# One masked product instead of two: sliding-window attention with unsplit weights, a difference of values, and squares in halves

## The chip, the core and the metric

The kernel runs on one core of a Trainium2 chip. A core has five engines with an instruction queue each, which run side by side and wait for one another through semaphores: TensorE (matrix products; PE in the profile, and PEld for its loading of weights), VectorE (DVE), ScalarE (ACT), GpSimd (POOL) and SyncE (SP), which issues most of the DMA transfers. The metric is the device time of one execution in microseconds, the median of several runs.

## The reference

One decoder layer on 2048 tokens of width 1024, in float32. A projection of the normed input gives queries (8 heads of 64), keys and values (2 shared heads of 64) and the input of a convolution group. Attention and convolution are put side by side, projected, normed and added to the input; a SwiGLU feed-forward with its own norms follows. The part that matters here is the attention, over a window of 128 with 128-token blocks:

```python
s = jnp.einsum("bnqhgd,bnkhd->bnhgqk", qb, kb) * scale      # 128 queries x 256 keys of a block
dist = qi + BLOCK - kj
in_band = (dist >= 0) & (dist < WINDOW)
s = jnp.where(valid, s + bias, -jnp.inf)
m = jnp.maximum(jnp.max(s, axis=-1, keepdims=True), sink)
p = jnp.exp(s - m)
denom = jnp.sum(p, axis=-1, keepdims=True) + jnp.exp(sink - m)
o = jnp.einsum("bnhgqk,bnkhd->bnqhgd", p / denom, vb)
```

For query q of a block, the keys in the band are those of the same block up to q and those of the block before it after q: exactly 128 keys, one for each key position 0 to 127. So a 128 x 128 matrix of weights per head holds all of them, with a key position k that belongs to the own block where k <= q and to the previous block where k > q. The norms are x times the reciprocal root of the mean of its squares over 1024 columns.

## The kernel before

The sequence is worked through in four tiles of 512 tokens (T = 512), each of four blocks of 128 (P = 128). Generators emit the work; a run loop advances a main generator and, with each step, pumps side lanes by a credit in estimated microseconds (`Lane`, from L1260 on). The final order on each engine is then made by the tile framework's scheduler, which works with its own timeline and with priorities, so an edit in one place may move instructions in others. Within an engine, instructions run in the order in which they stand.

The stages, with the letter that marks their tiles in the profile:
- `stage_a` (A): the projections, 14 units of 128 columns for each sequence tile. Products with float32 operands are made of three matmuls on a high and a low part, so each operand is split: ScalarE copies the high part (L133, L782), GpSimd or VectorE subtracts to get the low part (L135, L85). Weights of a unit arrive in a tile `raw` of two buffers. In the first sequence tile, a sum of squares (ScalarE L282 into `wx`, one buffer; VectorE adds; a product with `ones`) gives the norm, and row norms of later tiles are summed by ScalarE at L272. At the first of the four query units, the 512 values just projected are transposed on TensorE into a PSUM bank and copied to `vtok` (L415), which has five blocks: the last block of the previous sequence tile (L414) and the four of this one.
- `stage_b` (B): attention of a sequence tile, block by block. `front(b)` makes the scores of the 256 keys, folds the two key blocks into one 128 x 128 matrix per head with a predicated copy, adds the bias, takes the maximum, and ScalarE takes the exponentials (L478). `back(b)` multiplies by the reciprocal of the sum (VectorE), transposes the weights of four heads at a time (group g; TensorE L496), ScalarE copies them to `pg[:, 1]` (L497), and GpSimd selects twice (L499): keys after the query go to `pg[:, 0]`, and the others stay in `pg[:, 1]`, in place. Four products (the `mat` of L517) then add, in one PSUM bank, `pg[:, 1]` with the block's own values for both groups and `pg[:, 0]` with those of the previous block. The first block of the sequence has no previous one.
- taps and tail of the convolution (C): 480 scalar-tensor-tensor instructions on VectorE, in a lane of low priority, and transposes, norm and a small product.
- `stage_w` and `norm_w` (W): output projection and the two norms behind it. Each norm sums squares of four rows of 1024 with ScalarE (L738, L760), which writes the squares to a tile `junk` that nobody reads and the sum to a small tile; `rsqrt` follows on VectorE and, for three of the four, on GpSimd.
- H, F and G: the feed-forward with one level of a seven-product scheme. `stage_p2` (G) reads out PSUM on VectorE between its products; `finish` sums squares in halves of 512 (L1087).

Small vectors come from pools of 16 buffers that are named by the stage's letter (`sm`, L67).

Of the kernel before, what the change touches and what calls it, by code (L numbers as in the profile page):

```python
# [37 lines left out]
def layer_kernel(ctx, tc, x, xT, cols, rows, sinks, relb, onehot, w_in, w_pw, w_out, w_gate, w_up, w_down, out):  # L38
# [28 lines left out]
    def sm(n, dt=F32):  # L67
        kind = "A" if lab[0][0] == "G" else lab[0][0]
        return sb.tile([P, 8], dt, tag="sm" + kind, name=nm("sm"), bufs=16)[:, 0:n]
# [80 lines left out]
    def rsqrt(ssq, n, mean_over, beside_taps=True):  # L150
# [16 lines left out]
        return y  # L167

    def rsqrt_one(a, b):
        v, y, w, vs = (sm(1) for _ in range(4))  # L170
        stt(v, a, EPS, b, ALU.add, ALU.add)
        vts(y.bitcast(I32), v.bitcast(I32), 1, None, ALU.logical_shift_right)
        vts(y.bitcast(I32), y.bitcast(I32), -1, 0x5F3759DF, ALU.mult, ALU.add)
        vts(vs, v, -(2.0**-13), None, ALU.mult)
        for f, d in ((v, -3.0), (v, -12.0), (vs, 3 * 2.0**-5)):
            stt(w, y, f, y, ALU.mult, ALU.mult)
            stt(y, w, d, y, ALU.add, ALU.mult)
        return y
# [27 lines left out]
    for i in range(4):  # L206
# [5 lines left out]
        x0.append(xt)  # L212
    ones = cst.tile([P, 1], F32, name="ones")
    nc.vector.memset(ones, 1.0)
# [17 lines left out]

    neg = cst.tile([P, 1], F32, name="neg")
    nc.vector.memset(neg, NEG)
# [6 lines left out]
    nc.gpsimd.memset(kz[:, :, 0:P].bitcast(F32), 0.0)  # L241
    junk = cst.tile([P, D], BF16, name="junk")
    vtok = cst.tile([P, 5, P], F32, name="vtok")

# [19 lines left out]
    def row_norms(ts, tag):  # L264
        lab[0] = f"A{ts[0]}"
        n = 4 * len(ts)
        ssq = sm(n)
        for i in range(n):
            xt = f4(tag)
            r0 = ts[0] * T + i * P  # L270
            nc.sync.dma_start(xt, x[r0 : r0 + P])
            act(junk, xt, AF.Square, accum_out=ssq[:, i : i + 1])  # L272
        r = rsqrt(ssq, n, D)
        for j, t in enumerate(ts):
            rn[t] = r[:, 4 * j : 4 * j + 4]
# [51 lines left out]
    def stage_a(t, hn, before_kv, hooks, post=None):  # L327
# [79 lines left out]
        for i in range(4):  # L407
            oq = proj(10 + i)
            if i == 0:
                pv = mm()  # L410
                for s in range(4):
                    nc.tensor.transpose(pv[:, s * P : (s + 1) * P], vt[:, s * P : (s + 1) * P], ident)
                if t:
                    nc.vector.tensor_copy(vtok[:, 0], vtok[:, 4])  # L414
                nc.vector.tensor_copy(vtok[:, 1:5].rearrange("p a b -> p (a b)"), pv)  # L415
            qi = hl("ql")
# [13 lines left out]
    def stage_b(t):  # L430
# [54 lines left out]
        def back(b):  # L485
# [3 lines left out]
            for g in range(2):  # L489
# [7 lines left out]
                act(pg[:, 1], o, AF.Copy)  # L497
                for kb in range(1 if first else 0, 2):
                    nc.gpsimd.affine_select(  # L499
                        out=pg[:, kb].rearrange("p (i q) -> p i q", q=P),  # L500
                        in_=pg[:, 1].rearrange("p (i q) -> p i q", q=P),
                        compare_op=ALU.is_ge if kb else ALU.is_gt,
                        fill=0.0,
                        base=0,
                        pattern=[[0, 4], [1 if kb else -1, P]],
                        channel_multiplier=-1 if kb else 1,
                    )
# [6 lines left out]
            for kb in (1,) if first else (1, 0):  # L514
                for g in (1, 0):
                    sl = slice(64 * g, 64 * g + 64)
                    r = mat(o[sl], vtok[:, b + kb, sl], pt[g][:, kb], start=kb == 1, stop=first or kb == 0)  # L517
                    if lead is None:
                        lead = r
                    else:  # L520
                        after_first(lead, r)
# [111 lines left out]
    def stage_x():  # L633
        lab[0] = "X0"
        rel = cst.tile([32, 8], F32, name="rel")
        nc.sync.dma_start(rel, relb)
# [95 lines left out]
    def norm_w(w, spill, acc, mtag):  # L732
        L = f"W{w}"
        lab[0] = L
        gb = load_gb(0)
        ssq = sm(4)
        for s in range(4):
            act(junk, acc[s], AF.Square, accum_out=ssq[:, s : s + 1])  # L738
            yield 0.5
            lab[0] = L  # L740
        r = rsqrt(ssq, 4, D, w < 3)
        yield 3
        lab[0] = L
        ssq2 = sm(4)
        for s in range(4):
# [13 lines left out]
            nc.sync.dma_start(h_scr[r0 : r0 + P], acc[s])  # L759
            act(junk, acc[s], AF.Square, accum_out=ssq2[:, s : s + 1])  # L760
            yield 1.5
        lab[0] = L
        r2 = rsqrt(ssq2, 4, D, w < 3)
        yield 3
# [316 lines left out]
    def finish(L, gb, jobs, pool=True):  # L1081
# [3 lines left out]
        for j, (rows_, halves) in enumerate(jobs):  # L1085
            for n in range(2):
                act(junk[:, 0:T], halves[n], AF.Square, scale=D**-0.5, accum_out=ssq[:, 2 * n + j : 2 * n + j + 1])  # L1087
                vtt(halves[n], halves[n], gb[n], ALU.mult)
            yield 2.0
            lab[0] = L  # L1090
# [12 lines left out]
    def stage_p2(ws, am, td, last=False):  # L1103
# [60 lines left out]
        def scale_even(h):  # L1164
            for b in (2 * h, 2 * h + 1):
                lab[0] = L
                c = home("c11", "x", b)
                act(junk[:, 0:T], c, AF.Square, scale=D**-0.5, accum_out=sse[:, b : b + 1])
                ptt(c, c, gbs[0], ALU.mult)
# [68 lines left out]
        for b in range(4):  # L1238
# [3 lines left out]
            ssq = sm(1)  # L1242
            act(junk[:, 0:T], banks[b], AF.Square, scale=D**-0.5, accum_out=ssq)
            g = f2("fa")
# [245 lines left out]
```

## Time and profile before

| what | value |
|---|---|
| median of 3 runs | 2036.23 us (2028.73 to 2038.02) |
| profiled execution, its own time | 2033.91 us |
| its span, first to last instruction | 2032.2 us |
| mean granted TensorE clock | 0.987 |
| busy: TensorE, VectorE, ScalarE, GpSimd | 1959.0, 1504.8, 988.8, 382.4 us |

The attention lies between about 95 and 600 us of the span. A busy time is the sum of the engine's instructions and not yet a place on the path: since TensorE is busy for nearly all of the span, what the time depends on is where TensorE waits and for whom, and at what clock it runs. The rows that show it stand in the prediction. In a row of the timeline, the first numbers are start and duration in microseconds, and the brackets say how long the engine was idle before and what ended it.

### The profile page before, as it was taken

To read this page: it belongs to the slowest core of one execution; us is meant where nothing else is said; L and a number is where in the kernel's file an instruction comes from. 1 tells how busy PE (TensorE), PEld (TensorE's weight loads), DVE (VectorE), ACT (ScalarE), POOL (GpSimd) and SP (SyncE) were. 2 spreads that over 40 slices of the span, in tenths; PEclk is the share of its full clock that TensorE was granted. 3 is DMA by queue.
4 is the path that set the end of the run, shared out by engine and by line. 5 is a ranking of instruction groups with operands and counts; after the bars stand their busy time and mean duration, and the time that the engine had idled before them with its cause. 6 is when DMAs were issued, how large, how long until landed. Compare 5 with 4: busy or idle time off the path is not lost. (4 is left out here: it accounts for less than half of the span.)

```text
span 2032.2 us, 27181 instructions
## 1 busy us (share of the span) xinstructions
PE 1959.0 (96%) x8826; PEld 1566.8 (77%) x8826; DVE 1504.8 (74%) x2664; ACT 988.8 (49%) x1938; POOL 382.4 (19%) x447
## 2 busy tenths in 40 slices
PE   8999999998889989999989999989999999999998
PEld 7877767776667778788878878878788888888886
DVE  5999887993895889888649985576756665545557
ACT  5455445456546633333346457556643433345443
POOL 6011224423111300000001012102523233221000
PEclk9999999999999999999999999999999999999999
DMA  8786645568558876777376778589944443266554
GB/s 310 268 290 234 207 129 187 189 221 276 184 174 305 291 236 235 271 248 255 133 265 208 231 251 297 188 285 335 335 154 161 150 171 115 98 228 230 193 187 165
DMA packets 234110, 451.44 MB, mean 222 GB/s; under 512 B 23496, under 2 KB 49264, under 8 KB 233968
## 3 DMA queue, kind: packets, MB, share of 16 engines
q1 hardware_dynamic: 211184, 411.96, 60.7%
q10 hardware_dynamic: 20544, 30.42, 4.1%
q0 software_dynamic: 2240, 7.34, 0.9%
q8 instruction: 69, 1.13, 0.2%
q14 instruction: 73, 0.60, 0.1%
HBM read 330.60 MB, written 119.02 MB: 221 GB/s over the span
## 5 line engine op out<-in xcount | busy, mean ns | idle before, releaser
L85 DVE SCALAR_TENSOR_TENSOR fc@C<-glu@C,colt,fc@C 128x512 f32<-128x512 f32 x480 | 371.7, 788 | 3.0
L108 PE MATMUL mm@F<-hl@H,w@F 128*128 128x512 f32 x1056 | 254.3, 392 | 3.1 <-ACT mm@F L909 3.1
L108 PE MATMUL mm@G<-hl@G,hl@G 128*128 128x512 f32 x924 | 229.1, 398 | 6.0 <-DVE x@G L85 5.3
L108 PEld LDWEIGHTS mm@F<-hl@H,w@F 128*128 128x128 f32 x1056 | 198.8, 189 | 45.6 <-ACT mm@F L909 4.0
L108 PEld LDWEIGHTS mm@G<-hl@G,hl@G 128*128 128x128 f32 x924 | 174.9, 192 | 43.9 <-ACT hl@G L782 5.9
L108 PE MATMUL mm@A<-hl@A,w@A 128*128 128x512 f32 x840 | 205.8, 396 | 2.3 <-DVE hl@A L85 1.2
L782 ACT ACTIVATE w@F<-chl@F 128x512 fp32r<-128x512 f32 x220 | 135.5, 625 | 145.3 <-PE mm@F L108 139.7
L108 PE MATMUL mm@G<-w@G,hl@G 128*128 128x512 f32 x876 | 199.5, 389 | 0.0
L108 PEld LDWEIGHTS mm@G<-w@G,hl@G 128*128 128x128 f32 x876 | 164.4, 188 | 34.1
L108 PEld LDWEIGHTS mm@A<-hl@A,w@A 128*128 128x128 f32 x840 | 154.9, 188 | 37.4 <-DVE hl@A L85 3.1
L85 DVE TENSOR_TENSOR w@F<-chl@F,w@F 128x512 fp32r<-128x512 f32 x198 | 146.6, 742 | 38.8 <-ACT w@F L782 38.2
L108 PE MATMUL mm@F<-mid@H,w@F 128*128 128x512 f32 x528 | 133.7, 398 | 4.7 <-ACT mm@F L909 3.4
L108 PE MATMUL mm@F<-p@H,w@F 128*128 128x512 f32 x528 | 130.8, 393 | 0.3 <-ACT at@F L1031 0.3
L108 PE MATMUL mm@F<-ql@H,w@F 128*128 128x512 f32 x528 | 127.4, 390 | 2.5 <-ACT w@F L782 2.2
L108 PE MATMUL mm@F<-x@H,w@F 128*128 128x512 f32 x528 | 125.8, 391 | 1.5 <-ACT fa@F L931 1.5
L108 PEld LDWEIGHTS mm@F<-mid@H,w@F 128*128 128x128 f32 x528 | 100.1, 191 | 27.6 <-ACT mm@F L909 4.0
L108 PEld LDWEIGHTS mm@F<-ql@H,w@F 128*128 128x128 f32 x528 | 98.9, 188 | 23.9 <-ACT w@F L782 2.8
L108 PEld LDWEIGHTS mm@F<-p@H,w@F 128*128 128x128 f32 x528 | 100.0, 190 | 22.0 <-ACT at@F L1031 1.1
L108 PEld LDWEIGHTS mm@F<-x@H,w@F 128*128 128x128 f32 x528 | 98.7, 188 | 22.7 <-ACT fa@F L931 1.9
L133 ACT ACTIVATE w@A<-raw@A 128x512 fp32r<-128x512 f32 x110 | 67.3, 626 | 88.4 <-PE mm@A L108 46.5
L108 PE MATMUL mm@W<-w@W,hl@W 128*128 128x512 f32 x384 | 100.4, 405 | 8.3 <-ACT hl@W L704 6.3
L108 PE MATMUL tr@W<-w@W,ql@W 128*128 128x512 f32 x384 | 98.8, 396 | 6.0 <-ACT mid@W L675 4.8
(299 smaller groups left out, 3368.3 us busy)
## 6 DMA issues: line engine op xcount, KB each, us to landing
mids<-fa@F SPq DMA_DIRECT2D x154, 256.0 KB, 2.6
raw@A<-w_in SPq DMA_DIRECT2D x55, 512.0 KB, 4.5
w@A<-lo_in SPq DMA_DIRECT2D x84, 256.0 KB, 3.5
fc@G<-mids SPq DMA_DIRECT2D x77, 256.0 KB, 3.4
fa@G<-mids SPq DMA_DIRECT2D x75, 256.0 KB, 4.4
gb@F<-keeps SPq DMA_DIRECT2D x72, 256.0 KB, 4.3
raw@W<-w_out SPq DMA_DIRECT2D x32, 512.0 KB, 5.4
w@W<-lo_out SPq DMA_DIRECT2D x48, 256.0 KB, 3.8
```

The lines of the kernel that those rows point to most:

```text
L85: r = op(*args, **kw)
L108: r = nc.tensor.matmul(*args, **kw)
L133: act(w[:, 0], raw, AF.Copy)
L782: act(w[:, 0], x, AF.Copy)
```

## The change

- Attention: the transposed weights stay whole in `pg[:, 1]`, and only one select is left, of the keys after the query into `pg[:, 0]`. The products are: all weights with the block's own values, plus the selected weights with the difference of the previous block's values and the own ones. `vtok` shrinks to the four blocks of the tile, and `vdif` holds the four differences; the first of them is made from the last block of the previous tile.
- `norm_w`: each sum of squares is made in two halves of 512 columns, and a VectorE add joins the two sets of four sums. `junk` shrinks to 512 columns. The row norms write their squares over their own input, which nobody reads afterwards.
- Smaller moves: `ones` and `neg` share a tile, `rel` becomes one of the small vectors, and these of stage X come from the pool of A.

```diff
     def sm(n, dt=F32):
-        kind = "A" if lab[0][0] == "G" else lab[0][0]
+        kind = "A" if lab[0][0] in "GX" else lab[0][0]
...
+    def squares(row, to, s):
+        for n in range(2):
+            act(junk, row[:, n * T : (n + 1) * T], AF.Square, accum_out=to[:, 4 * n + s : 4 * n + s + 1])
+
+    def joined(s):
+        o = sm(4)
+        vtt(o, s[:, 0:4], s[:, 4:8], ALU.add)
+        return o
...
-    ones = cst.tile([P, 1], F32, name="ones")
+    ones_neg = cst.tile([P, 2], F32, name="ones_neg")
+    ones, neg = ones_neg[:, 0:1], ones_neg[:, 1:2]
...
-    junk = cst.tile([P, D], BF16, name="junk")
-    vtok = cst.tile([P, 5, P], F32, name="vtok")
+    junk = cst.tile([P, T], BF16, name="junk")
+    vtok = cst.tile([P, 4, P], F32, name="vtok")
+    vdif = cst.tile([P, 4, P], F32, name="vdif")
...
             nc.sync.dma_start(xt, x[r0 : r0 + P])
-            act(junk, xt, AF.Square, accum_out=ssq[:, i : i + 1])
+            act(xt, xt, AF.Square, accum_out=ssq[:, i : i + 1])
...
                 if t:
-                    nc.vector.tensor_copy(vtok[:, 0], vtok[:, 4])
-                nc.vector.tensor_copy(vtok[:, 1:5].rearrange("p a b -> p (a b)"), pv)
+                    nc.vector.tensor_copy(vdif[:, 0], vtok[:, 3])
+                nc.vector.tensor_copy(vtok.rearrange("p a b -> p (a b)"), pv)
+                if t:
+                    vtt(vdif[:, 0], vdif[:, 0], vtok[:, 0], ALU.subtract)
+                vtt(vdif[:, 1:], vtok[:, 0:3], vtok[:, 1:], ALU.subtract)
...
                 act(pg[:, 1], o, AF.Copy)
-                for kb in range(1 if first else 0, 2):
+                if not first:
                     nc.gpsimd.affine_select(
-                        out=pg[:, kb].rearrange("p (i q) -> p i q", q=P),
+                        out=pg[:, 0].rearrange("p (i q) -> p i q", q=P),
                         in_=pg[:, 1].rearrange("p (i q) -> p i q", q=P),
-                        compare_op=ALU.is_ge if kb else ALU.is_gt,
+                        compare_op=ALU.is_gt,
                         fill=0.0,
                         base=0,
-                        pattern=[[0, 4], [1 if kb else -1, P]],
-                        channel_multiplier=-1 if kb else 1,
+                        pattern=[[0, 4], [-1, P]],
+                        channel_multiplier=1,
                     )
...
-                    r = mat(o[sl], vtok[:, b + kb, sl], pt[g][:, kb], start=kb == 1, stop=first or kb == 0)
+                    r = mat(o[sl], vtok[:, b, sl] if kb else vdif[:, b, sl], pt[g][:, kb], start=kb == 1, stop=first or kb == 0)
...
-        rel = cst.tile([32, 8], F32, name="rel")
+        rel = sm(8)[0:32]
...
-        ssq = sm(4)
+        ssq = sm(8)
         for s in range(4):
-            act(junk, acc[s], AF.Square, accum_out=ssq[:, s : s + 1])
+            squares(acc[s], ssq, s)
             yield 0.5
             lab[0] = L
-        r = rsqrt(ssq, 4, D, w < 3)
+        r = rsqrt(joined(ssq), 4, D, w < 3)
...
-            act(junk, acc[s], AF.Square, accum_out=ssq2[:, s : s + 1])
+            squares(acc[s], ssq2, s)
             yield 1.5
         lab[0] = L
-        r2 = rsqrt(ssq2, 4, D, w < 3)
+        r2 = rsqrt(joined(ssq2), 4, D, w < 3)
```

More of the change, by code (lines that the diff above doesn't have):

```diff
@@ L231, in layer_kernel @@
     h_scr = dr.tile([S, D], F32, name="h_scr")
-    neg = cst.tile([P, 1], F32, name="neg")
     nc.vector.memset(neg, NEG)
@@ L735, in norm_w @@
         gb = load_gb(0)
-        ssq = sm(4)
+        ssq = sm(8)
         for s in range(4):
-            act(junk, acc[s], AF.Square, accum_out=ssq[:, s : s + 1])
+            squares(acc[s], ssq, s)
             yield 0.5
             lab[0] = L
-        r = rsqrt(ssq, 4, D, w < 3)
+        r = rsqrt(joined(ssq), 4, D, w < 3)
         yield 3
         lab[0] = L
-        ssq2 = sm(4)
+        ssq2 = sm(8)
         for s in range(4):
@@ L1086, in finish @@
             for n in range(2):
-                act(junk[:, 0:T], halves[n], AF.Square, scale=D**-0.5, accum_out=ssq[:, 2 * n + j : 2 * n + j + 1])
+                act(junk, halves[n], AF.Square, scale=D**-0.5, accum_out=ssq[:, 2 * n + j : 2 * n + j + 1])
                 vtt(halves[n], halves[n], gb[n], ALU.mult)
@@ L1167, in scale_even @@
                 c = home("c11", "x", b)
-                act(junk[:, 0:T], c, AF.Square, scale=D**-0.5, accum_out=sse[:, b : b + 1])
+                act(junk, c, AF.Square, scale=D**-0.5, accum_out=sse[:, b : b + 1])
                 ptt(c, c, gbs[0], ALU.mult)
@@ L1242, in stage_p2 @@
             ssq = sm(1)
-            act(junk[:, 0:T], banks[b], AF.Square, scale=D**-0.5, accum_out=ssq)
+            act(junk, banks[b], AF.Square, scale=D**-0.5, accum_out=ssq)
             g = f2("fa")
```

## The prediction

> **What bounds the kernel now.** I read the page's shares of busy time first, then the waits of TensorE, then the windows and the timeline around the largest of them.
>
> ```profile
> span 2032.2 us, 27181 instructions
> PE 1959.0 (96%) x8826; PEld 1566.8 (77%) x8826; DVE 1504.8 (74%) x2664; ACT 988.8 (49%) x1938; POOL 382.4 (19%) x447
> ```
> TensorE is busy for 1959.0 of 2032.2 us. Its instructions stay the same in number and shape here, so only two things can move the time: the 73 us in which it idles, and stretches in which its granted clock is low. The waits of TensorE (us in total, times, longest) say who holds it:
>
> ```profile
> PE tr@B L108 <- POOL p@B L499: 10.4, 4, 6.8
> PE mm@F L108 <- ACT mm@F L909: 6.5, 4, 2.5
> PE mm@W L108 <- ACT hl@W L704: 6.3, 5, 3.0
> PE mm@G L108 <- DVE x@G L85: 5.3, 1, 5.3
> ```
> The largest is the one that the change touches: the product of weights and values waits for GpSimd's selects. Two of its four waits hold nearly all of it (instructions in order of time; start, duration, engine):
>
> ```profile
> 277.80 0.60 PE L496 MATMUL tr@B<-ident,p@B 128*128 128x128 f32 x4
> 283.43 0.57 ACT L497 ACTIVATE p@B<-tr@B 128x512 f32<-128x512 f32 x1
> 284.08 1.71 POOL L499 TENSOR_SCALAR_AFFINE_SELECT p@B<-p@B 128x512 f32<-128x512 f32 x2 [5.84 <-ACT p@B L497]
> 285.83 2.81 PE L108 MATMUL tr@B<-p@B,vtok 128*64 128x512 f32 x8 [3.08 <-POOL p@B L499]
> ```
> ```profile
> 453.96 0.49 PE L496 MATMUL tr@B<-ident,p@B 128*128 128x128 f32 x3
> 455.52 1.08 ACT L497 ACTIVATE p@B<-tr@B 128x512 f32<-128x512 f32 x2
> 456.19 7.50 POOL L499 TENSOR_SCALAR_AFFINE_SELECT p@B<-p@B 128x512 f32<-128x512 f32 x4 [5.45 <-ACT p@B L497]
> 456.75 1.29 DVE L85 TENSOR_TENSOR x@W<-fa@W,x@W 128x512 f32<-128x512 f32 x2
> 457.95 1.22 DVE L85 TENSOR_TENSOR x@W<-wx@W,x@W 128x1024 f32<-128x1024 f32 x1
> 463.74 3.68 PE L108 MATMUL tr@B<-p@B,vtok 128*64 128x512 f32 x8 [6.77 <-POOL p@B L499]
> ```
> Transposes, ScalarE's copy, the selects, then the product: in the first case the copy comes late, in the second four selects take 7.50 us. A long wait costs a second time, through the clock (window, TensorE busy, ..., granted clock in the third column from the end):
>
> ```profile
> 1750.00:1800.00 50.00, 50.00 (x223) 41.39 (x222) 22.12 (x30) 19.59 (x36) 12.97 (x10) 1.00 0.35 121
> 286.00:292.00 6.00, 6.00 (x27) 2.95 (x26) 5.89 (x7) 2.42 (x4) 2.91 (x2) 0.72 0.57 181
> 464.00:468.00 4.00, 4.00 (x13) 1.02 (x12) 0.92 (x2) 3.04 (x8) 1.27 (x1) 0.54 1.02 406
> ```
> An undisturbed matmul takes 50/223 = 0.224 us. Behind the two waits the clock is 0.72 for 6 us and 0.54 for 4 us: 1.7 + 1.8 = 3.5 us lost.
>
> **The change, part by part.**
>
> *Selects and the wait.*
> ```profile
> L499 POOL TENSOR_SCALAR_AFFINE_SELECT p@B<-p@B 128x512 f32<-128x512 f32 x62 | 59.5, 968 | 214.0 <-ACT p@B L497 212.7
> L499 POOL TENSOR_SCALAR_AFFINE_SELECT p@B<-p@B x62: 632/868/5287, 129.4 to 592.2; 128x512 f32<-128x512 f32 x62
> ```
> 32 of 62 selects go (31 us of GpSimd, off the path). What counts: the first two of the four products now need ScalarE's copy alone, the last two one select per group instead of two. The order of the built programs also moves: counting the instructions between a block's last transpose and its product at 0.224 us, most blocks had 7 to 10 us of other TensorE work there and now have 5 to 7; the two bad ones go from 4.3 to 6.7 us (286) and from 2.5 to 5.9 us (464), up to the masked pair. So, by the rows above: at 286 the copy ends at 284.0 and one select of 0.86 at 284.9; the masked pair stands at 278.4 + 6.7 = 285.1: no wait. At 464 the four selects took 7.50; three at the median 0.74 leave 5.3 for the first (the group's maximum), so the second group's one select ends at about 456.2 + 5.3 + 0.7 = 462.2, and the pair stands at 454.45 + 5.9 = 460.4: 1.8 us of wait stay. A block that had cover enough before loses some:
>
> ```profile
> 368.74 0.60 PE L496 MATMUL tr@B<-ident,p@B 128*128 128x128 f32 x4
> 375.38 0.58 ACT L497 ACTIVATE p@B<-tr@B 128x512 f32<-128x512 f32 x1
> 376.04 1.67 POOL L499 TENSOR_SCALAR_AFFINE_SELECT p@B<-p@B 128x512 f32<-128x512 f32 x2 [1.78 <-ACT p@B L497]
> ```
> Its unsplit pair stands 6.1 us behind 369.3, at 375.4, and the copy ends at 376.0: 0.6 us. The other blocks give about 1.0 us together. Taken: -10.4 + (1.8 + 0.6 + 1.0) = -7.0, and since no wait over 3 us is left, -3.5 of clock. Bounds: 0 (all waits come back) and -13.9.
>
> The Trainium skill (TensorE: Matmul & The Clock Gate, "What's actually happening") says that the array falls to half clock after an idle window of about 3.4 us and returns after as long a busy one. The trace agrees at 464 (0.54), but shows a drop at 286 already behind 3.08 us. By the rule that second drop was chance and the clock term would be 1.8 instead of 3.5.
>
> *The difference of values.*
> ```profile
> L415 DVE COPY vtok<-mm@A x4: 680/688/692, 82.5 to 468.6; 128x512 f32<-128x512 f32 x4
> L414 DVE COPY vtok<-vtok x3: 212/220/220, 90.9 to 386.4; 128x128 f32<-128x128 f32 x3
> ```
> Per sequence tile one subtract of 384 columns (between 0.22 and 0.69; 0.55) and one of 128 (0.22) from the second tile on: 2.9 us of VectorE. The copy keeps its place, and so does its wait for the previous tile's last product, in front of the taps in VectorE's queue. The first product comes 60 us behind the first copy, so nothing reaches TensorE: 0 (at most +2.9).
>
> *Squares in halves.*
> ```profile
> 24.62 1.04 ACT L272 ACTIVATE junk<-p@A 128x1024 bf16<-128x1024 f32 x1
> 25.78 1.06 ACT L272 ACTIVATE junk<-p@A 128x1024 bf16<-128x1024 f32 x1
> 1365.89 0.63 ACT L1087 ACTIVATE junk<-p@G 128x512 bf16<-128x512 f32 x1
> 1366.64 0.63 ACT L1087 ACTIVATE junk<-x@G 128x512 bf16<-128x512 f32 x1
> ```
> A whole row takes 1.16 from start to start, two halves 2 x 0.75 = 1.50: 32 rows add 10.9 us to a ScalarE that is 49% busy. In each of the eight sums the first half can run before the row's second half is there, so the tail is 0.43 shorter, and a VectorE add of four columns joins (0.1 to 0.4). Bounds: -3.4 and +13.5 (all of it in front of the ScalarE copies that hold mm@F for 6.5 us). Taken: 0, as ScalarE's idle half is nearest. The in-place square of the row norms and the merged or shortened constants do the same work: 0.
>
> *Order at the start.* The built order puts the third projection's weight load behind the last x tile in SP's queue, ScalarE's split of it behind the first gate's tanh, and the sum over ones 12 matmuls (2.7 us) earlier.
>
> ```profile
> 19.82 0.33 SPq L143 DMA_DIRECT2D raw@A<-w_in  x1
> 23.65 1.06 ACT L282 ACTIVATE wx@A<-x@X 128x1024 f32<-128x1024 f32 x1 [3.97 <-DVE gb@A L85]
> 24.74 0.38 SPq L257 DMA_DIRECT2D x@A<-xT  x1
> 30.23 1.15 ACT L133 ACTIVATE w@A<-raw@A 128x512 fp32r<-128x512 f32 x2 [2.12 <-DMA raw@A<-w_in]
> 34.51 0.63 ACT L352 ACTIVATE fa@A<-fa@A 128x512 f32<-128x512 f32 x1 [1.20 <-DVE fa@A L85]
> ```
> The x tile waits for the square at 23.65, so the load moves from 19.82 to 25. The split would end at 34.51 + 0.63 + 0.57 = 35.7, or 33.0 if the whole norm chain moves up by 2.7; TensorE wanted it at 32.4. Bounds 0 and +3.3; taken 33.0 - 32.4 = +0.6, as the chain moves with its first matmul.
>
> *Order in the third norm.*
> ```profile
> 1347.36 0.69 DVE L85 TENSOR_TENSOR mid@W<-at@W,mid@W 128x512 f32<-128x512 f32 x1 [0.46 <-DMA at@W<-x]
> 1349.17 2.47 DVE L85 TENSOR_TENSOR x@G<-x@G,mm@G 128x512 f32<-128x512 f32 x4
> ```
> The read-out that holds TensorE for 5.3 us stands behind an add that waits for its x load. In the new order three of the four read-outs stand in front of that add: -(0.46 + 0.6) = -1.0 (bounds -5.3 and +1).
>
> **Sum.** The profiled execution took 2033.9 us: -10.4 + 3.4 - 3.5 + 0.6 - 1.0 = -10.9, so 2023.0. The median of the runs (2036.2) stands 2.3 above it; so 2025.3 for a median. 0.5% of it, 10.2 us, is about what a measurement of this kernel can tell from no change.
>
> **The rivals.**
> *The wait comes back.* The scheduler puts the product about 2 us nearer to its transposes, just what one select saves. For it: the four selects of 7.50 us began beside VectorE's adds, which stay; against it: the covers at the two bad places grew. Then some 3 of the 10.9 us remain: 2033, no change. The Trainium skill (SBUF — State Buffer, "Who interferes with whom") has a VectorE instruction with two SBUF inputs and a GpSimd one exclude each other for their whole length; the trace agrees at 456, and by that the remaining select stays as slow as the first was.
>
> *The start costs its full bound* (+3.3, and a clock drop of 1.7): 2025.3 + 2.7 + 1.7 = 2030, no change.
>
> *Softmax becomes late: slower.* Scores and transposes of the attention blocks stand up to 17 us earlier in the new TensorE order, beside a VectorE that is full:
> ```profile
> 350.00:400.00 50.00, 50.00 (x242) 37.27 (x241) 49.78 (x103) 19.76 (x51) 22.09 (x24) 1.00 0.57 181
> 447.73 1.72 DVE L85 TENSOR_TENSOR p@B<-p@B,sm@B 128x512 f32<-128x512 f32 x2
> 453.19 0.38 PE L496 MATMUL tr@B<-ident,p@B 128*128 128x128 f32 x2
> ```
> At 453 the weights were ready 3.7 us ahead of their transposes, and the new order takes 3.4 of them. Four blocks are that tight. If each waits as long as the longest select (5.3, and 1.7 of clock), that is +28, with the gain kept 2025.3 + 28 = 2053. From 21 us on, three of the four, it is slower by over 0.5%. Against it: the other twelve have 6 us and more, and the normalising multiply moves up in VectorE's queue too.
>
> **How the numbers follow.** Forecast 0.47: 2025.3. What would lose part of it stands in the rivals, so its own range reaches mostly down: 4.3 less if the norm's wait goes whole, 3.4 less if no wait for selects stays; 2017 to 2027, nearly all of it under the 0.5% bound (2026.0). The wait comes back 0.25, the start 0.10, softmax 0.18. Faster 0.45, same 0.36 (the two middle rivals and a sliver of the first), slower 0.19. The range 2015 to 2042 takes in the forecast's gain ends, both rivals of no change and a softmax case of two late blocks (2025.3 + 14), and leaves out most of that case beyond it.
>
> **What would show it.** GpSimd's selects x30 near 29 us; TensorE's wait for them 2 to 5 us instead of 10.4; granted clock 1.00 behind the products at 286 and 464; ScalarE some 11 us busier. A wait of TensorE at about 31 to 35 us for the split of the third weights would show the start term. The prediction fails if transposes of weights (L509 afterwards) wait for VectorE, or if the waits for ScalarE in the norms grow beyond 6.5.

## The result and the profile after

The changed kernel takes 2043.74 us (median of 6 runs, 2041.87 to 2047.25) against 2035.66 us of the kernel before beside it. The ratio is 1.0042, with a 95% interval of 1.0028 to 1.0055: slower by some 8 us, where 10 us faster had been forecast.

The page of the changed kernel, its first part:

```profile
span 2043.5 us, 27208 instructions
PE 1971.7 (96%) x8826; PEld 1569.2 (77%) x8826; DVE 1496.9 (73%) x2679; ACT 996.0 (49%) x2002; POOL 353.9 (17%) x415
```
The span grew by 11.3 us; the two profiled executions, of 2033.9 and 2045.2 us, lie somewhat further apart than the medians. TensorE's idle time, span minus busy, is 71.8 us against 73.2 before, so it did not grow. Its busy time did, by 12.7 us, with the same 8826 matmuls of the same shapes.

Those waits of TensorE in the changed kernel on which the argument bears (us in total, times, longest):

```profile
PE mm@F L108 <- ACT mm@F L922: 8.7, 5, 2.2
PE mm@G L108 <- ACT junk L171: 4.5, 1, 4.5
PE tr@B L108 <- ACT ql@A L436: 4.2, 1, 4.2
PE tr@X L108 <- DMA mb@X<-b_scr: 3.0, 1, 3.0
PE mm@W L108 <- ACT hl@W L717: 2.9, 3, 2.0
PE mm@A L108 <- ACT w@A L133: 2.6, 1, 2.6
PE tr@B L509 <- DVE p@B L85: 2.1, 1, 2.1
PE tr@B L108 <- POOL p@B L512: 0.4, 1, 0.4
```
The wait for the selects, 10.4 us before, is down to 0.4: the step that the change was argued from came out better than forecast. Other waits stand in its place: for ScalarE's scaled queries at 469 us (4.2), for the bias table (3.0) and the third weights (2.6) at the start, and for the normalised weights (2.1).

The busy time is the larger matter. Here is TensorE's timeline of the changed kernel where the scores of the third sequence tile begin, and the same scores in the kernel before (start, duration, what, how many matmuls):

```profile
326.65 0.73 PE L108 MATMUL tr@B<-kz,ql@A 64*128 64x256 f32 x6
327.31 0.49 PE L108 MATMUL mm@A<-mid@A,w@A 128*128 128x512 f32 x1
327.73 0.39 PE L108 MATMUL tr@B<-kz,ql@A 64*128 64x256 f32 x2
328.05 0.50 PE L108 MATMUL mm@A<-mid@A,w@A 128*128 128x512 f32 x1
328.48 0.38 PE L108 MATMUL tr@B<-kz,ql@A 64*128 64x256 f32 x1
328.79 0.50 PE L108 MATMUL mm@A<-mid@A,w@A 128*128 128x512 f32 x1
329.22 0.38 PE L108 MATMUL tr@B<-kz,ql@A 64*128 64x256 f32 x1
329.53 0.50 PE L108 MATMUL mm@A<-mid@A,w@A 128*128 128x512 f32 x1
```
```profile
330.89 1.15 PE L108 MATMUL tr@B<-kz,ql@A 64*128 64x256 f32 x13
334.99 5.30 PE L108 MATMUL mm@W<-w@W,hl@W 128*128 128x512 f32 x16 [2.95 <-ACT hl@W L704]
```
Before, 13 score matmuls (those that read `kz`: 64 rows, in pairs on the two halves of the rows) take 1.15 us in one piece. After, single ones alternate with full matmuls of the projection: from 328.05 to 328.79 to 329.53, one score and one projection matmul take 0.74 us. The projection matmul alone takes 0.224, and a score within a run 0.06 (half of the median distance from one pair to the next). Some 0.46 us of the 0.74 is neither work nor a recorded wait; the page counts it as busy. The place shows how the time is lost, and not a net loss: before, TensorE stood idle for 2.95 us behind the unbroken run, and here full matmuls fill the time.

Counted over the whole trace, TensorE's order has 87 unbroken runs of score matmuls where it had 67, and 30 runs of the products of weights and values where it had 24. What a run of scores between full matmuls costs can be read from the distances between starts in the kernel before, at full clock and without a wait: from the full matmul ahead of it to the second one behind it, a run of one score takes 0.45 us more than the same matmuls take unbroken (the median of 12 places), and a run of six or more 0.40 (12 places). The expectations below divide the 0.40 into 0.306 to leave a run and 0.093 to come back. Over the whole trace, the distances between starts at and next to the ends of runs of both kinds, at full clock, exceed the usual ones by 27.9 us before and 37.3 after: 9.4 of the 12.7 us by which the busy time grew.

### The profile page after: what moved, and what is told of

The parts are those of the page before. It is cut to its first block, busy times and chain, and to the rows that moved or that the text cites. A ratio compares the mean times of both kernels' runs of the same rounds, so it can differ in the third digit from the quotient of the medians.

```text
span 2043.5 us, 27208 instructions
## 1 busy us (share of the span) xinstructions
PE 1971.7 (96%) x8826; PEld 1569.2 (77%) x8826; DVE 1496.9 (73%) x2679; ACT 996.0 (49%) x2002; POOL 353.9 (17%) x415
```

## The experiments

Three theories were set against each other at first. *Start*: the time is lost by the late bias table and the late third weights. *Halves*: it is lost in ScalarE's queue by the squares in halves. *Order*: any edit makes the scheduler deal a new order, in which gains and losses fall anywhere. From the traces of the first four runs came a fourth, *pieces*: what is lost is the price of broken runs, and it can be counted.

All the kernels with their ratio to the kernel before, the runs of scores and of products, and for their profiled execution TensorE's busy and idle time. "Slow clock" is the sum, over windows of 5 us, of 5 us times what the granted clock lacks to 1.

| kernel | ratio, 95% interval | runs: scores, products | busy | idle | slow clock |
|---|---|---|---|---|---|
| before | 1 | 67, 24 | 1959.0 | 73.2 | 27.1 |
| after | 1.0042 (1.0028 to 1.0055) | 87, 30 | 1971.7 | 71.8 | 28.5 |
| e1 start back, flawed | 1.0052 (1.0032 to 1.0071) | 81, 30 | 1972.7 | 76.8 | 30.3 |
| e2 attention part only | 1.0099 (1.0074 to 1.0123) | 74, 31 | 1975.5 | 76.2 | 41.9 |
| e3 start edits only | 1.0010 (0.9997 to 1.0023) | 67, 24 | 1959.3 | 77.8 | 23.8 |
| e4 halves only | 1.0027 (1.0009 to 1.0045) | 69, 24 | 1959.6 | 72.4 | 25.7 |
| e5 after, scores held together | 1.0119 (1.0100 to 1.0138) | 49, 27 | 1964.1 | 91.4 | 40.6 |
| e6 before, scores held together | 1.0159 (1.0137 to 1.0180) | 44, 21 | 1964.6 | 98.4 | 49.5 |
| e7 before, pairs swapped | 1.0069 (1.0051 to 1.0087) | 81, 34 | 1973.4 | 72.6 | 27.5 |
| e9 after, old start | 1.0029 (1.0014 to 1.0044) | 77, 33 | 1972.7 | 69.5 | 32.1 |
| e10 after, masked pair first | 1.0075 (1.0048 to 1.0102) | 79, 23 | 1971.8 | 76.4 | 39.9 |
| e11 both | 1.0023 (1.0006 to 1.0041) | 76, 23 | 1965.6 | 72.0 | 27.8 |
| e12 e2, masked pair first | 1.0019 (1.0005 to 1.0034) | 72, 23 | 1963.9 | 69.0 | 28.1 |
| e13 after, other pace | 1.0156 (1.0141 to 1.0171) | 106, 41 | 1988.9 | 79.3 | 32.3 |
| e14 before, other pace | 1.0034 (1.0021 to 1.0048) | 85, 35 | 1974.2 | 67.9 | 28.5 |
| e15 e11, other pace | 1.0043 (1.0028 to 1.0059) | 68, 19 | 1961.8 | 78.0 | 30.8 |
| e16 e11, other rate | 1.0060 (1.0040 to 1.0079) | 71, 19 | 1968.2 | 81.3 | 37.1 |

None is faster than the kernel before. Each ratio is against executions of the kernel before from the same session, with medians from 2034.8 to 2038.4 us. Busy and idle time are those of one execution, which can lie up to 9 us from the kernel's median (e4).

### The parts alone (e1 to e4)

e1 undoes the start, with the scratch tiles taken from elsewhere:

```diff
-        rel = sm(8)[0:32]
+        rel = junk.bitcast(F32)[0:32, 0:8]
...
-            act(xt, xt, AF.Square, accum_out=ssq[:, i : i + 1])
+            act(vdif.bitcast(BF16).rearrange("p a b -> p (a b)"), xt, AF.Square, accum_out=ssq[:, i : i + 1])
```


> The changed kernel, with the start as it was: rel lies in the (still unused) scratch of the squares instead of a slot of the small tiles, and the squares of the row norms go into the (still unused) tile of differences instead of back over the rows. Theory start: the 7 us that the changed kernel lies behind at 115 us are the late bias table and the late third weights; then this runs at 2036 to 2038, 6 to 8 us below the changed kernel, without the 3.0 us wait of tr@X at 65 us and without the 2.6 us wait of mm@A at 33 us. Theory halves (the squares in halves cost the time in ScalarE's queue): 2042 to 2045, with the two waits gone or not. Theory order (every edit reorders all that follows, and what is won in one place is lost in the next): anywhere within 5 us of the changed kernel, with other waits later.

It took 2044.78 us. The scratch was badly chosen: row norms of later sequence tiles are summed from 95 to 116 us, when the first differences, written at 91, are already there. The squares overwrite them, and the output is not the layer's. The wait of `tr@X` did go, but the time is not that of the start alone; e9 repeats it cleanly.

e2 is the attention part alone. So that it fits, the squares over whole rows are stored as bytes:

```diff
-    junk = cst.tile([P, T], BF16, name="junk")
+    wide = cst.tile([P, D], I8, name="junk")
+    junk = wide.bitcast(BF16)
...
-            act(xt, xt, AF.Square, accum_out=ssq[:, i : i + 1])
+            act(wide, xt, AF.Square, accum_out=ssq[:, i : i + 1])
```


> The attention part of the change alone: unsplit weights times own values plus the masked part times the difference, with the squares over whole rows (their results, which nobody reads, are stored as one byte each so that a row fits) and the start as before. Theory start: the wait for the selects goes (10.4 us) and nothing is paid at the start, so 2025 to 2030, faster than before. Theory halves: the same, 2025 to 2030. Theory order: the selects' wait goes, but other waits in the attention stretch take its place, so 2034 to 2040.

It took 2054.09 us, the slowest of the first four, with the old start and no halves. Both theories on the parts are refuted for the whole of the loss. Its idle time is only 3 us above that of before; 16.5 us are in the busy time, and a good part of that is slow clock:

```profile
330.00:335.00 5.00, 1.80 (x17) 1.10 (x14) 4.84 (x15) 0.88 (x2) 0.00 (x0) 0.97 0.67 156
335.00:340.00 5.00, 2.97 (x7) 2.39 (x8) 2.96 (x6) 1.57 (x3) 0.00 (x0) 0.50 0.85 299
345.00:350.00 5.00, 0.76 (x13) 0.56 (x11) 5.00 (x10) 3.74 (x18) 1.15 (x2) 0.83 0.14 52
350.00:355.00 5.00, 5.00 (x12) 3.94 (x13) 5.00 (x11) 2.58 (x6) 1.88 (x2) 0.50 0.11 9
```
In these windows (TensorE's busy time is the second number, the granted clock the third from the end) TensorE is busy 1.80 and 0.76 us of 5, and the clock in the next window is 0.50.

e3 is the kernel before with the start edits:

```diff
-        rel = cst.tile([32, 8], F32, name="rel")
+        rel = sm(8)[0:32]
...
-            act(junk, xt, AF.Square, accum_out=ssq[:, i : i + 1])
+            act(xt, xt, AF.Square, accum_out=ssq[:, i : i + 1])
```


> The kernel before with the start edits alone (rel in a slot of the small tiles, ones and neg in one tile, row-norm squares in place); two masked products and whole-row squares as before. Theory start: 6 to 8 us slower than before, 2042 to 2044, with a wait of tr@X of about 3 us near 65 us. Theory halves: 2035 to 2037. Theory order: slower by 7 at 115 us, but anywhere from 2030 to 2046 at the end.

It took 2038.96 us, 3 us more; the interval just reaches 1. Behind equal TensorE work its trace lies 4.0 us behind that of before at 66 us and 4.9 at 120, and the idle time is 4.6 us larger. So the start costs some 3 to 5 us, half of what theory start asked for. The mechanism shows in the timelines where SP issues the load of `rel`, in before and after:

```profile
9.92 0.34 SPq L636 DMA_DIRECT2D rel<-relb  x1
```
```profile
25.37 0.42 SPq L649 DMA_DIRECT2D sm@X<-relb  x1
...
65.22 2.42 PE L108 MATMUL tr@X<-mb@X,fa@X 128*128 128x512 f32 x4 [2.98 <-DMA mb@X<-b_scr]
```
```profile
65.00:70.00 5.00, 4.78 (x11) 3.02 (x12) 4.93 (x9) 1.43 (x3) 0.00 (x0) 0.66 0.97 361
```
As a vector of the pool, `rel` is loaded 15 us later, the bias table made from it comes later, and in the changed kernel TensorE stands for 2.98 us and then runs at 0.66 (the window in the third fence). In e3 itself this wait is 0.7 us, and that for the third weights 2.6 as in the changed kernel.

e4 is the kernel before with the halves alone:

```diff
-            act(junk, acc[s], AF.Square, accum_out=ssq[:, s : s + 1])
+            squares(acc[s], ssq, s)
...
-        r = rsqrt(ssq, 4, D, w < 3)
+        r = rsqrt(joined(ssq), 4, D, w < 3)
```


> The kernel before with the 32 squares of the output projection's norms in halves, and nothing else. Theory halves: slower by 5 to 10 us, 2041 to 2046, with TensorE's waits for ScalarE's copies of mm@F grown from 6.5 to over 10 us. Theory start: within 2 us of before, 2034 to 2038, as the prediction has it (0, bounds -3.4 and +13.5). Theory order: within 5 us of before, with waits moved in every stage behind the first norm (from about 380 us on).

It took 2042.62 us, slower by 1.0009 to 1.0045. The profiled execution is one of two near 2033.7 us while most others lie between 2040 and 2045, and it shows waits for `mm@F` shrunk and not grown. That the halves cost some 5 us (2 to 9 by the interval) is measured; where they do is not shown.

Together the parts alone cost 3, 5 and 20 us and the whole change 8. Effects that do not add up speak for the order, and for something in it that is not tied to a part.

### Holding the scores together, breaking them up, and the price of a break (e5 to e8)

e5 and e6 add one dependency without a semaphore, in the changed kernel and in the kernel before:

```diff
         r = nc.tensor.matmul(*args, **kw)
         if not inlane[0]:
+            if glue[0] is not None:
+                after_first(glue[0], r)
+                glue[0] = None
             lead_pe[0] = r
...
                             if len(lead) < 2:
                                 lead.append(r)
+                glue[0] = r
```


> The changed kernel, with one order added: the next projection matmul in program order stands behind the last score matmul of its group of twelve. The score matmuls then stand in 49 unbroken runs in TensorE's order instead of 87 (67 before), the products in 27 instead of 30 (24 before). Theory pieces (each break of a run of scores costs some 0.40 us, 0.306 to leave it and 0.093 to come back, read from the distances of starts in the traces of before and after): 38 x 0.40 + some for the products = 15 us less than the changed kernel, 2026 to 2031. Theory order (waits only move about): within 5 us of the changed kernel, 2039 to 2049. Theory clock (the loss is slow clock behind long waits, of which holding things together makes more): above 2044.

> The kernel before with the same added order and nothing else: 44 runs of scores instead of 67, 21 runs of products instead of 24. Theory pieces: 23 x 0.40 + 0.5 = 10 us less than before, 2024 to 2029. Theory order: within 5 us of before. Theory clock: slower than before.

They took 2058.30 and 2065.51 us, the opposite of what theory pieces expected. The waits of e5 say why (us in total, times, longest):

```profile
PE tr@B L109 <- DVE sm@B L477: 23.7, 10, 5.0
PE mm@F L109 <- ACT mm@F L927: 10.5, 9, 2.2
```
A score group needs a PSUM bank that VectorE has read, and now the projections behind it wait for that too: 23.7 us of new waits, and 12 us more slow clock from them. The busy time of e5 did fall, by 7.6 us in spite of that; that of e6 rose by 5.6, with 22 us more slow clock and 26.5 us of the same waits. So the breaks are not idle waste: a run is left because VectorE is late, and the full matmul put in its place is cover. A wait of 2 to 5 us costs more than a break.

e7 breaks the kernel before, by issuing its two masked pairs in the opposite order:

```diff
-            for kb in (1,) if first else (1, 0):
+            for kb in (1,) if first else (0, 1):
...
-                    r = mat(o[sl], vtok[:, b + kb, sl], pt[g][:, kb], start=kb == 1, stop=first or kb == 0)
+                    r = mat(o[sl], vtok[:, b + kb, sl], pt[g][:, kb], start=first or kb == 0, stop=kb == 1)
```


> The kernel before with the two masked pairs of the product of weights and values issued in the opposite order (previous keys first). The arithmetic is the same, but the built order breaks the scores into 81 runs instead of 67 and the products into 34 instead of 24. Theory pieces: some 12 us slower than before, 2043 to 2050, most of it in TensorE's busy time. Theory order: within 5 us of before. Theory clock: as the waits fall, no more busy time than the granted clock explains.

It took 2048.29 us, 13.5 more than before, as theory pieces had it: busy time up by 14.4 us, idle time and slow clock as before. The busy line of its page and one line of its waits:

```profile
PE 1973.4 (96%) x8826; PEld 1566.5 (77%) x8826; DVE 1504.9 (74%) x2664; ACT 986.2 (48%) x1938; POOL 382.6 (19%) x447
```
```profile
PE tr@B L108 <- POOL p@B L499: 2.8, 1, 2.8
```
It also has all 62 selects, and its wait for them is 2.8 us instead of 10.4. So the wait that the prediction built on was itself a matter of the order.

e8 measures a break by itself; its plan of stretches (how often, kind, how many in a row, full matmuls behind them):

```python
plan = [(1, "score", 0, 100)]
for times in (12, 4, 2, 1):
    plan += [(96 // times, "score", times, times), (1, "score", 0, 100)]
for times in (4, 2, 1):
    plan += [(96 // times, "pv", times, 2 * times), (1, "score", 0, 100)]
```


> No layer at all (its output is not the layer's): TensorE alone, with the forms of the layer's matmuls on one tile. Seven stretches, each behind 100 full matmuls (128x512, fp32r): four with 96 score matmuls (64 rows, 256 columns, in pairs for the two halves of the rows) and 96 full ones, alternating by 12, 4, 2 and 1 (8, 24, 48 and 96 runs); three with 96 value matmuls (64 output rows, 512 columns, fp32, in pairs) and 192 full ones, alternating by 4, 2 and 1 (24, 48 and 96 runs). Theory pieces: the four score stretches differ by 0.40 us a run: 6, 16 and 35 us more than the first. The rivals: no difference over 2 us between the first three, since what the traces show at the ends of runs would be semaphores and late inputs; alternating by 1 may cost in any case, as the two halves of a pair then no longer run side by side.

The windows of its seven stretches, cut where each begins and ends, and one of full matmuls alone:

```profile
32.13:65.10 32.97, 32.97 (x193) 24.45 (x193) 0.00 (x0) 0.00 (x0) 0.00 (x0) 0.85 0.00 0
90.27:129.04 38.77, 38.77 (x193) 23.92 (x193) 0.00 (x0) 0.00 (x0) 0.00 (x0) 0.85 0.00 0
154.22:201.94 47.72, 47.72 (x194) 23.62 (x194) 0.00 (x0) 0.00 (x0) 0.00 (x0) 0.85 0.00 1
227.12:342.46 115.34, 115.34 (x194) 53.91 (x194) 0.49 (x1) 0.00 (x0) 0.00 (x0) 0.51 0.00 0
369.65:473.00 103.35, 103.35 (x385) 47.14 (x385) 0.00 (x0) 0.00 (x0) 0.00 (x0) 0.85 0.00 0
498.19:609.33 111.14, 111.14 (x385) 42.74 (x385) 0.00 (x0) 0.00 (x0) 0.00 (x0) 0.85 0.00 0
634.52:807.11 172.59, 172.59 (x386) 47.73 (x385) 1.16 (x2) 0.00 (x0) 0.00 (x0) 0.85 0.00 0
...
66.00:88.00 22.00, 22.00 (x90) 16.88 (x89) 0.00 (x0) 0.00 (x0) 0.00 (x0) 0.85 0.00 1
```
The same 96 score and 96 full matmuls take 32.97 us in 8 runs, 38.77 in 24 and 47.72 in 48: (38.77 - 32.97) / 16 = 0.36 us and (47.72 - 38.77) / 24 = 0.37 us a run. A full matmul takes 0.244 us here (22.00 / 90 in the last row) and 0.224 in the layer. The expectations below scale the price with it, to 0.33 us in the layer; the layer's own distances, 0.40 and 0.45, do not bear that out.

For products it is (111.14 - 103.35) / 24 = 0.32 us, as long as pairs stay whole; one by one, a further break costs (172.59 - 111.14) / 48 = 1.28 us. There the two halves of a pair, which otherwise start within 0.01 us of each other, are held apart; how much of the 1.28 that explains is not shown.

The fourth stretch ran mostly at half clock, so its total can't be compared. But in its first 3 us, up to 231, the clock was still 0.85, and from one full matmul to the next, with one score between, it takes 0.74 us: as at 327 us in the changed kernel, here with no other engine to wait for. Of the 87 runs of scores in the changed kernel, 39 are single scores like these; before, it was 26 of 67.

The Trainium skill (TensorEngine Tiling (Array Packing), "Key Properties") says that changing the tiling mode drains TensorE. The runs agree in so far as each change of form costs time; that a drain takes it, no trace shows. I had not looked for it, since the change adds no matmul.

### The start once more, and the masked pair first (e9 to e12)

e9 restores the start cleanly (the scratch of e2, with the halves kept). e10 leaves the start and issues the masked pair ahead of the unsplit one, by the same edit as in e7:

```diff
-                    r = mat(o[sl], vtok[:, b, sl] if kb else vdif[:, b, sl], pt[g][:, kb], start=kb == 1, stop=first or kb == 0)
+                    r = mat(o[sl], vtok[:, b, sl] if kb else vdif[:, b, sl], pt[g][:, kb], start=first or kb == 0, stop=kb == 1)
```
e11 is both, and e12 is e2 with the masked pair first.

> The changed kernel with the start as it was, this time with a scratch that nobody else uses (the row norms' squares are stored as single bytes in the scratch of the halves, rel lies in that scratch before it is used). Built order: 77 runs of scores instead of 87, 33 runs of products instead of 30. Theory start: 2043.7 less the 3 to 5 us which the start edits cost alone (e3), so 2038 to 2041, without the waits at 33 and 65 us. Theory pieces adds some 2 us of gain (10 runs of scores fewer at 0.33 us, three of products more): 2036 to 2039. Theory order: waits and slow clock in the attention stretch move, and decide: 2035 to 2052.

> The changed kernel with the masked pair (weights times differences) issued ahead of the unsplit pair, so that both pairs wait for the one select, as they did for the first select before. Built order: 79 runs of scores instead of 87, 23 of products instead of 30. Theory pieces: 8 x 0.33 + 7 x 0.33 = 5 us less busy time (up to 7 by the distances in the traces), 2037 to 2039 if no wait for the selects comes back. Theory select (the unsplit pair first is what covers the select): the wait for selects comes back by some 5 us and takes that gain away, 2042 to 2046.

> Both edits of the two runs before it at once: the changed kernel with the old start and the masked pair first. 76 runs of scores, 23 of products. Theory start and pieces together: 2043.7 - 4 - 6 = 2034, between 2030 and 2038. Theory order: anywhere in 2034 to 2052, with the sum of the two edits not the sum of their effects.

> The attention part of the change alone (as in e2: old start, squares over whole rows stored as single bytes), with the masked pair first. 72 runs of scores instead of e2's 74 and before's 67; 23 of products instead of 31 and 24. Theory pieces: 10 runs fewer than e2, some 3 to 4 us less busy time. The 15 us of slow clock that e2 has over before hang on its own long waits in the attention stretch (330 to 355, 470 to 480, 530 to 540, 960 us); if these are chance of the built order, this lands at 2030 to 2045; if they belong to the difference of values, at 2048 to 2054.

e9 took 2041.83 us: a ratio lower than that of the changed kernel by 1.3 in a thousand, within both intervals. The start's waits went and slow clock of 3.6 us came. e10 took 2050.17, above what either of its theories expected, with 2.7 us of waits for the selects back and 11 us more slow clock; its busy time is that of the changed kernel in spite of 15 fewer runs. e11, at 2039.76, is better than either, where the sum of the two edits' effects would be about 2048. And e12 took 2038.94 where e2 took 2054.09: the same arithmetic, with two pairs swapped, is 8 in a thousand apart. So e2's slow clock was a chance of the built order and does not belong to the difference of values.

### The order without the change (e13 to e16)

Over these thirteen kernels of the layer (before, after, and all runs but e8), a fit of TensorE's busy time by least squares gives 1906.3 us + 0.59 x slow clock + 0.37 x runs of scores + 0.59 x runs of products, and it misses none of them by more than 2.0 us. The price of a run of products is uncertain: the fit's standard error is 0.10 (0.04 for scores), and e8 found 0.32 for whole pairs, as which they stand in the layer. The last four were to test it on orders that it had not seen. They alter only pacing numbers of the attention lane; e13 (changed kernel) and e14 (kernel before):

```diff
-    RC0, RC1, RC2, RC3, RW0, RW, RB, LC = 0.7, 1.1, 0.4, 0.9, 1.7, 1.25, 0.8, 100
+    RC0, RC1, RC2, RC3, RW0, RW, RB, LC = 0.7, 1.1, 0.4, 0.9, 1.7, 1.25, 0.9, 100
...
-    YC = 3
+    YC = 2
```
e15 is e11 with `YC = 4` and `YP = 2.5`, e16 is e11 with `RB` at 0.65.

> The changed kernel with two pacing numbers of the attention lane altered (rate RB 0.9 instead of 0.8, gap YC 2 instead of 3), so that the same instructions are built in another order: 106 runs of scores and 41 of products instead of 87 and 30. Theory pieces, with 0.37 us a run of scores and 0.59 us a run of products: 19 x 0.37 + 11 x 0.59 = 13.5 us more busy time, 2055 to 2059. Theory change (the time belongs to the arithmetic of the change, not to the order): within 4 us of the changed kernel.

> The kernel before with the same two pacing numbers altered and nothing of the change: 85 runs of scores and 35 of products instead of 67 and 24. Theory pieces: 18 x 0.37 + 11 x 0.59 = 13 us more busy time, 2045 to 2051: the loss of the changed kernel, without the change. Theory change: within 4 us of before.

> The changed arithmetic with the old start, the masked pair first and two gaps of the attention lane altered (YC 4, YP 2.5): 68 runs of scores and 19 of products. Theory pieces: busy 1906.3 + 0.59 x 28 of slow clock + 68 x 0.37 + 19 x 0.59 = 1959, as before; with the 70 us of idle time that all unheld kernels have, a span of 2029 and a time of 2030 to 2034, level with before or slightly ahead. Theory change: 2038 to 2044, as the five kernels with the changed arithmetic and the old or new start so far.

> As the run before it, with the rate of the attention lane at 0.65 instead of 0.8 and the two gaps as they were: 71 runs of scores and 19 of products. Theory pieces: one us more busy time than the run before it, 2031 to 2035. Theory change: 2038 to 2044.

The busy times by the fit, with the slow clock that each run showed, and as measured: 1988.4 and 1988.9 for e13, 1974.9 and 1974.2 for e14, 1960.5 and 1961.8 for e15, 1965.3 and 1968.2 for e16. The first line below is e13's, the second e14's, and the third is a line of e14's waits:

```profile
PE 1988.9 (96%) x8826; PEld 1571.5 (76%) x8826; DVE 1493.9 (72%) x2679; ACT 995.7 (48%) x2002; POOL 347.2 (17%) x415
```
```profile
PE 1974.2 (97%) x8826; PEld 1570.2 (77%) x8826; DVE 1499.0 (73%) x2664; ACT 988.2 (48%) x1938; POOL 375.8 (18%) x447
```
```profile
PE tr@B L108 <- POOL p@B L499: 0.2, 1, 0.2
```
e14 (2044.47 us) has nothing of the change and is slower than before by 1.0021 to 1.0048, as the changed kernel is by 1.0028 to 1.0055; its wait for the selects fell to 0.2 us all the same. Its busy time grew by 15.2 us, but its time by only 6.0 (2038.43 before beside it) and not by the 13 of theory pieces; in the profiled execution 5.3 us of idle time went. What the changed kernel gains and loses, a new order alone can bring.

The times of the other three, 2069.53, 2045.25 and 2050.22 us, came out above what either theory expected, through the part that the fit doesn't hold. e13 has 79.3 us of idle time where 71.8 was assumed, and 3.8 us more slow clock. e15, with as few runs as before and nearly its busy time, has 78.0:

```profile
PE mm@W L108 <- ACT hl@W L718: 11.6, 5, 5.4
```
Before had 6.3 us of these waits for ScalarE's copies in the output projection. So the runs give TensorE's busy time, and not the time of a new order, of which the waits are a part. Whether the changed arithmetic in its best order would be level with before is open: e12 (1.0005 to 1.0034) is the nearest, and no run shows it faster.

## Why the prediction was wrong, point by point

- **The step that failed** stands at its beginning: "Its instructions stay the same in number and shape here, so only two things can move the time: the 73 us in which it idles, and stretches in which its granted clock is low." There is a third: which matmul stands next to which. With the fit's prices, 20 more runs of scores and 6 more of products make 20 x 0.37 + 6 x 0.59 = 10.9 us, and 1.4 us more slow clock another 0.8: 11.7 of the 12.7 us by which the busy time grew (20 x 0.40 + 6 x 0.32 = 9.9 by the prices measured alone, and 9.4 read directly). The changed order was known, and it was read only for how much cover it leaves the selects. The price stood in the trace of before:

```profile
488.59 0.38 PE L108 MATMUL tr@B<-kz,ql@A 64*128 64x256 f32 x1
488.90 0.50 PE L108 MATMUL mm@W<-w@W,hl@W 128*128 128x512 f32 x1
489.33 0.38 PE L108 MATMUL tr@B<-kz,ql@A 64*128 64x256 f32 x1
489.64 0.49 PE L108 MATMUL mm@W<-w@W,hl@W 128*128 128x512 f32 x1
```
  Two full matmuls 0.74 us apart with one score between them, in a stretch without a wait.
- **Selects and the wait**: -10.4 + 3.4 was forecast, and -10.0 came. But e7 and e14 lose most of this wait with all their selects, so the removal of the selects is not shown to be the cause. In the working, "the median 0.74" of a select is 0.87 in the row above it; the first select took the 5.3 us all the same.
- **Clock, -3.5**: wrong. The clock behind the products that stood at 286 and 464 us is 1.00, as forecast, but the slow clock of the whole went from 27.1 to 28.5 us. "Since no wait over 3 us is left" looked only at the selects; the waits that came at 65 us (2.98) and 469 us (4.2 in the list of waits) each drew a slow stretch of their own.
- **What would be late next** at the end of the third query projection was not named. It was ScalarE's scaled query, which the scores at 469 us wait for.
- **Start, +0.6 (bounds 0 and +3.3)**: mis-sized, and one part was missed. The split of the third weights held TensorE for 2.6 us. The rest came from "the merged or shortened constants do the same work: 0": `rel` does the same work 15 us later. Alone, the start edits cost 3 us (e3), and the changed kernel lies 7 us behind by 115 us; putting them back gained less than the measurement can tell (e9).
- **Squares in halves, 0 (bounds -3.4 and +13.5)**: alone they cost about 5 us (e4), inside the bounds, at a place not found. ScalarE is 7 us busier, not 11. The waits for ScalarE at `mm@F`, 6.5 us before, grew to 8.7, which the prediction gave as a sign that it fails; but e3, without halves, has 8.0, and e4, with them, 4.6, so this is not shown to come from the halves.
- **Third norm, -1.0**: near in size, but not for the reason given. Three read-outs do stand in front of the add now, and the wait went from 5.3 to 4.5 us. But it is for ScalarE's squares now, and e4, the halves alone, has the same wait of 4.3.
- **Difference of values, 0**: nothing in the waits shows it. e12 bounds the attention part with the old start by 1.0005 to 1.0034.
- **The rivals**: none had the mechanism. "Softmax becomes late" came to 2.1 us of waits for normalised weights, far from its 28; that transposes of weights wait for VectorE at all was the other sign of failure that the prediction gave. "The wait comes back" did not happen, and its time was mis-added: 10.9 less the 7.0 of the wait and the 3.5 of clock that hang on it leaves 0.4, not 3. The measured time lies 1.7 us above the upper end of the range, which took in its cases by waits alone.

## What to carry to other kernels

Where matmuls on part of the array's rows or columns share TensorE with full ones, count the unbroken runs in the built order of both kernels and price the difference. Here prices fitted to thirteen kernels, with the slow clock that each run showed, gave TensorE's busy time within 3 us in four orders that the fit had not seen; a price read from distances of starts in one trace, 0.40, came close to the fit's 0.37 for scores. The time of the kernel takes the waits besides. Forcing the runs together is no cure if another engine sets when they can start: e5 and e6 paid more in waits than they saved in breaks. And where a scheduler makes the order, run one edit that changes only the order (e14) before an effect of a half per cent is put down to the arithmetic.

## What was not expected of the hardware

- In e8 TensorE had no gap for 825 us, and its granted clock stood at 0.85 from 10 us on, with a full matmul at 0.244 us. In the layer, with its waits, it is 1.00 most of the time. The runs don't show why.
- The stretch of e8 that alternates one score with one full matmul ran at 0.50 for most of its 115 us, though TensorE is recorded as busy throughout:

```profile
225.00:230.00 5.00, 5.00 (x17) 2.81 (x15) 0.00 (x0) 0.00 (x0) 0.00 (x0) 0.85 0.02 3
230.00:235.00 5.00, 5.00 (x11) 2.45 (x10) 0.00 (x0) 0.00 (x0) 0.00 (x0) 0.59 0.00 0
235.00:240.00 5.00, 5.00 (x9) 2.29 (x8) 0.00 (x0) 0.00 (x0) 0.00 (x0) 0.50 0.00 0
```
  What sets the clock is then not only idle time as the profile records it. In the changed kernel the alternation at 327 us lasts 4.4 us, and the granted clock of that window is 1.00.
- The wait of 2.98 us at the start was followed by a clock of 0.66, so here a drop set in behind a wait of under 3 us too. The wait of 2.95 us at 332 to 335 us in the kernel before was followed by 0.70 over 5 us.
